# Ten products of a zero tile instead of twenty, and a later, lower-ranked norm chain for half evictions, in a one-layer encoder kernel

## The chip, the core and the metric

One core of a Trainium2 chip runs the whole kernel. The metric is device time in microseconds (us), median of several executions. TensorE (PE) multiplies, VectorE (DVE) and ScalarE (ACT) do the elementwise work, GpSimd (POOL) adds a few tiles and issues accumulating DMAs, SyncE (SP) issues nearly all loads and stores.

## What is computed

One layer with two residual sub-layers, over 512 tokens and 2048 channels. In short:

```python
h = rms_norm(x, norm_gains[0])
parts = split(h @ w_in, 11)             # four head groups: two attentions, a recurrence, a short conv
mixed = concatenate([y_sb, y_df, y_lru, y_sc]) @ w_out
x = x + rms_norm(mixed, norm_gains[1])
h = rms_norm(x, norm_gains[2])
x = x + rms_norm(conv_geglu_ffn(h, w_up, conv_w, w_down), norm_gains[3])
```

`rms_norm` needs, for every token, the sum of squares over all 2048 channels. All data is float32; each product is made of three (or two wider) products of a rounded part `hi` and a rest `lo`.

## The kernel before

Activations lie with channels on the 128 partitions and tokens along the free axis, so a tile holds 128 channels by 512 tokens, or 256 for a half of the tokens. `group` (a helper, lines 133 to 187) multiplies one group of four output blocks by all 2048 input channels, in eight chunks of 256 channels. Each chunk's weights come by one DMA into `w_raw` (three buffers), ACT rounds them into `w_hi` (L106), DVE writes the rest into `w_lo` (L107); `w_hi` and `w_lo` have three buffers each, so the work for chunk c waits for PE to be through with chunk c-3. The PE order is the program order. The order of the other engines is set by a scheduler from the program order and priorities: what stands under `tc.high_priority` (weights, and what `group` calls as `evac`) goes before all else; what an `evac` returns is called by `group` behind it without that priority.

Beside the products, `at(block, fn)` puts small work on a clock that `tick` advances four times in a chunk. PE takes its part of such work exactly at that place.

Places that the change and the prediction speak of:

- **Start.** After twenty products of the zero tile `idle` (L72, two passes each), group 0 of the input projection starts with L128 to L130. Meanwhile ACT and DVE split x (L199, L200) and the first weights. Squares of x (L282) are added up by DVE into `vd` (L284, L286, sixteen tiles); `norm0` (L308) takes the sum through PE at block 28, just ahead of the last chunk of the first group. Tiny instructions on `la_m` and others (L375 to L401) prepare constants on DVE.
- **Output projection.** `out_group` runs groups 0 and 1 over all 512 tokens, then groups 2 and 3 for the first 256 tokens (half 0), then groups 2 and 3 for half 1. PSUM has two pools of four banks, `mm` and `pa`. Its `evac` copies a finished bank out (L968 for full width; L978 and L979 for a half), squares it (L838, POOL adds up) and scales it (L964).
- **The norm chain of a half.** After the last half block, `residual` follows a few blocks later: L852 sums the squares through PE, L207 to L213 make the reciprocal root, L876 multiplies by it, and two accumulating DMAs (L878) and L882 add it to x. Then squares (L894, summed by L896), scalings (L902) and stores of x (L904, on SP), and some blocks later `norm2`: L911 on PE, L207 to L213, L917, and the splits L196/L197 into the input of the up projection of the same half (`up_plain`).

ACT, DVE, POOL and SP each work strictly in their order, so an ACT square (L894) that waits for an accumulating DMA also holds up the weight roundings (L106) behind it.

## Time and profile before

| | us |
|---|---|
| median of 3 executions (1743.55 to 1744.21) | 1743.61 |
| the profiled execution | 1741.86 |
| its span, first to last instruction | 1740.1 |
| PE busy in it | 1730.1 |
| DVE busy | 1253.8 |
| ACT busy | 905.8 |
| POOL busy | 157.8 |

The span is the time between the first and the last instruction on the chip; 1.76 us lie around it. PE is busy in all but 10 us of it. Busy time alone does not say what PE could do in less: a stretch of products is also read by its starts, since ends are modelled.

### The profile page before, as it was taken

The numbers are of one execution on the slowest core, as the hardware profiler recorded it, in microseconds if no ns is written. First come the engines' busy times: TensorE is split into PE (matmuls) and PEld (weight loads), VectorE is DVE, ScalarE is ACT, GpSimd is POOL, SyncE is SP. The second block draws the span as 40 slices with busy tenths as digits, with TensorE's granted clock in tenths as the row PEclk, the third lists the DMA queues.
The fourth block names the chain that finished last, engine by engine and source line by source line (L and its number), as shares of the span: only waits on it lengthen the run. The fifth ranks groups of instructions, "written<-read, shape, count | busy, mean of one in ns | idle before, by whom it ended". The sixth has DMA issues, their size and how long they took to land.

```text
span 1740.1 us, 24385 instructions
## 1 busy us (share of the span) xinstructions
PE 1730.1 (99%) x9168; PEld 1482.5 (85%) x9168; DVE 1253.8 (72%) x1949; ACT 905.8 (52%) x1367; POOL 157.8 (9%) x227
## 2 busy tenths in 40 slices
PE   9999999999999999999999999999999999999998
PEld 8778888888888888899988888888888888888886
DVE  7885587666556425799898988888878887776335
ACT  6443577665334334776655555555555573334342
POOL 0000011100000011100011111111111001110120
PEclk9999999999999999999999999999999999999999
DMA  7224222242223625775789888888888768888322
GB/s 258 84 99 147 92 79 79 79 158 97 85 86 97 230 97 181 233 234 180 208 230 243 236 224 247 225 230 223 228 239 226 210 198 232 217 201 296 102 91 97
DMA packets 96014, 304.43 MB, mean 175 GB/s; under 512 B 10356, under 2 KB 14708, under 8 KB 95896
## 3 DMA queue, kind: packets, MB, share of 16 engines
q1 hardware_dynamic: 79768, 245.19, 42.1%
q0 software_dynamic: 15552, 56.63, 17.4%
q8 instruction: 72, 1.18, 0.3%
q10 hardware_dynamic: 576, 1.05, 0.2%
q14 instruction: 46, 0.38, 0.1%
HBM read 262.45 MB, written 21.24 MB: 163 GB/s over the span
## 4 chain that ended last, share of the span: by engine, by line
PE 92%; DVE 3%; DMA 2%; ACT 2%; issue 1%; SPq 0%; POOL 0%; ACTq 0%; DVEq 0%; POOLq 0%
PE mm L164 32%; PE mm L1113 27%; PE mm L1118 14%; PE pa L164 5%; PE pa L156 2%; PE mm L128 2%; PE mm L130 2%; PE mm L129 2%; PE mm L156 1%; PE pa L611 1%; DMA w_raw<-in_w_out_dram 1%; DVE w_lo L107 1%; DVE vd L286 1%; PE pa L718 1%; ACT w_hi L106 0%
## 5 line engine op out<-in xcount | busy, mean ns | idle before, releaser
L107 DVE TENSOR_TENSOR w_lo<-w_raw,w_hi 128x1024 fp32r<-128x1024 f32 (+1 forms) x195 | 238.5, 1224 | 234.6 <-PE mm L164 117.3
L106 ACT CAST w_hi<-w_raw 128x1024 fp32r<-128x1024 f32 (+1 forms) x195 | 203.5, 1044 | 264.0 <-PE mm L164 174.1
L164 PE MATMUL mm<-a,w_hi 128*128 128x512 f32 (+1 forms) x1504 | 338.2, 375 | 0.0
L164 PEld LDWEIGHTS mm<-a,w_hi 128*128 128x128 f32 x1504 | 266.7, 188 | 50.9 <-issue 1.8
L1113 PE MATMUL mm<-a,w_hi 128*128 128x512 f32 x1088 | 272.6, 392 | 0.0
L1081 ACT CAST w_hi<-w_raw 128x1024 fp32r<-128x1024 f32 x145 | 152.3, 1050 | 196.0 <-PE mm L1113 154.9
L1113 PEld LDWEIGHTS mm<-a,w_hi 128*128 128x128 f32 x1088 | 195.6, 189 | 35.3 <-issue 0.2
L1082 DVE TENSOR_TENSOR w_lo<-w_raw,w_hi 128x1024 fp32r<-128x1024 f32 x145 | 177.0, 1221 | 29.9 <-ACT w_hi L1081 29.3
L164 PE MATMUL mm<-a,w_lo 128*128 128x512 f32 (+1 forms) x752 | 180.4, 377 | 0.0
L1118 PEld LDWEIGHTS mm<-a,w_lo 128*128 128x128 f32 x1088 | 148.4, 190 | 10.6
L1118 PE MATMUL mm<-a,w_lo 128*128 128x256 f32 x1088 | 151.7, 282 | 0.0
L164 PEld LDWEIGHTS mm<-a,w_lo 128*128 128x128 f32 x752 | 131.8, 189 | 22.3
L1113 PE MATMUL mm<-xs,w_hi 128*128 128x512 f32 x576 | 144.3, 392 | 0.2 <-DVE ub L1179 0.2
L1081 ACT CAST w_hi<-mg 128x1024 fp32r<-128x1024 f32 x82 | 85.6, 1044 | 85.0 <-PE mm L1113 82.5
L1113 PEld LDWEIGHTS mm<-xs,w_hi 128*128 128x128 f32 x576 | 103.6, 189 | 19.0 <-DVE ub L1179 0.4
L1082 DVE TENSOR_TENSOR w_lo<-mg,w_hi 128x1024 fp32r<-128x1024 f32 x82 | 100.1, 1220 | 21.4 <-ACT w_hi L1081 21.4
L1113 PE MATMUL mm<-mg,w_hi 128*128 128x512 f32 x352 | 88.1, 392 | 0.0
L1118 PEld LDWEIGHTS mm<-xs,w_lo 128*128 128x128 f32 x576 | 78.6, 190 | 5.6
L1179 DVE TENSOR_TENSOR ub<-ub,mm 128x256 f32<-128x256 f32 x196 | 81.2, 414 | 0.0
L1118 PE MATMUL mm<-xs,w_lo 128*128 128x256 f32 x576 | 80.3, 282 | 0.0
L1281 DVE TENSOR_TENSOR m<-m,mm 128x256 f32<-128x256 f32 x112 | 46.5, 416 | 37.0 <-PE mm L1118 37.0
L1113 PEld LDWEIGHTS mm<-mg,w_hi 128*128 128x128 f32 x352 | 63.3, 189 | 11.3
(332 smaller groups left out, 2709.1 us busy)
## 6 DMA issues: line engine op xcount, KB each, us to landing
w_raw<-in_w_up_dram SPq DMA_DIRECT2D x115, 512.0 KB, 5.3
w_raw<-in_w_in_dram SPq DMA_DIRECT2D x87, 512.0 KB, 3.4
mg<-in_w_up_dram SPq DMA_DIRECT2D x54, 512.0 KB, 4.4
w_raw<-in_w_out_dram SPq DMA_DIRECT2D x48, 512.0 KB, 3.6
w_raw<-in_w_dn_dram SPq DMA_DIRECT2D x32, 512.0 KB, 4.2
mg<-in_w_up_dram POOLq DMA_DIRECT2D x27, 512.0 KB, 7.8
w_raw<-in_w_up_dram POOLq DMA_DIRECT2D x27, 512.0 KB, 8.9
w_raw<-mg POOLq DMA_DIRECT2D x27, 512.0 KB, 6.0
```

Source lines behind the costliest of these rows:

```text
L106: w_split.append(A.copy(out=hi[:, sl], in_=raw[:, sl]))
L107: V.tensor_tensor(out=lo[:, sl], in0=raw[:, sl], in1=hi[:, sl].bitcast(F32), op=ALU.subtract)
L128: T.matmul(ps, lhsT=sh, rhs=mh, start=first, stop=False)
L129: T.matmul(ps, lhsT=sh, rhs=ml, start=False, stop=False)
L156: T.matmul(pss[u][:, 0:256] if low else pss[u].rearrange("p (a t) -> p a t", a=2), lhsT=(wh, wl)[low][:, kk, us], rhs=both[k][:, 0, ts] if ...
L164: T.matmul(pss[u], lhsT=a, rhs=b, start=c == 0 and kk == 0 and not low and i == 0, stop=False)
L1081: w_split.append(A.copy(out=by4(hi), in_=v))
L1082: V.tensor_tensor(out=by4(lo), in0=v, in1=by4(hi).bitcast(F32), op=ALU.subtract)
L1113: T.matmul(ps.rearrange("p (a t) -> p a t", a=2), lhsT=hi[:, k * P:(k + 1) * P], rhs=tops[name][k], start=first and k == 0, stop=False, **kw)
L1118: T.matmul(ps[:, 0:256], lhsT=lo[:, k * P:(k + 1) * P], rhs=tops[name][k][:, 0], start=False, stop=k == 7, **kw)
L1179: taken.append(V.tensor_tensor(out=t, in0=t, in1=ps[:, 256:512], op=ALU.add))
L1281: V.tensor_tensor(out=t, in0=t, in1=part, op=ALU.subtract if i else ALU.add)
```

## The change

The program multiplies the zero tile ten times, not twenty. Group 1 of the output projection puts its sums into the four `pa` banks, not into the `mm` banks that group 0 has just used. For half blocks only the copy and the addition (L978, L979) stay in the high-priority part; squaring and scaling move into a function that `evac` returns and that is ranked in program order. `residual` comes 8 blocks after the last block, not 6, and `norm2` 44 blocks after `residual`, not 43, with the squares and scalings between them at the same distance from `residual` as before.

```diff
-    for _ in range(20):
+    for _ in range(10):
         T.matmul(ps, lhsT=idle, rhs=idle, start=True, stop=True)
...
-            at(clock[0] + 43, lambda: norm2(hf, acc))
+            at(clock[0] + 44, lambda: norm2(hf, acc))
...
                     sum_of(m, ps)
-                    last = ss1[hfs[0]].add(m)
-                    A.activation(out=m, in_=m, func=AF.Copy, scale=gain(1, k))
-                    if last:
-                        at(clock[0] + 6, lambda: residual(hfs[0]))
+
+                    def more():
+                        last = ss1[hfs[0]].add(m)
+                        A.activation(out=m, in_=m, func=AF.Copy, scale=gain(1, k))
+                        if last:
+                            at(clock[0] + 8, lambda: residual(hfs[0]))
+                    return more
...
         for g in range(2):
-            out_group(g, (0, 1), ALL, mm_tile)
+            out_group(g, (0, 1), ALL, pa_tile if g else mm_tile)
```

The scheduler answers with another order in three places. (Lines after L963 carry numbers that are two or three higher in the changed kernel.)

DVE, ahead of `norm0`, the last additions of squares into `vd`; L107 is the rest of the tenth chunk's weights (the second chunk of group 1). Before:

```order
L286 TENSOR_TENSOR vd<-vd,t_446 128x512
L386 TENSOR_TENSOR la_m<-la_m,la_q 128x4
L286 TENSOR_TENSOR vd<-vd,t_485 128x512
L387 TENSOR_SCALAR la_m<-la_m 128x4
L286 TENSOR_TENSOR vd<-vd,t_488 128x512
L386 TENSOR_TENSOR la_m<-la_m,la_q 128x4
L107 TENSOR_TENSOR w_lo<-w_raw,w_hi 128x1024
```

Now:

```order
L286 TENSOR_TENSOR vd<-vd,t_436 128x512
L386 TENSOR_TENSOR la_m<-la_m,la_q 128x4
L107 TENSOR_TENSOR w_lo<-w_raw,w_hi 128x1024
L286 TENSOR_TENSOR vd<-vd,t_475 128x512
L387 TENSOR_SCALAR la_m<-la_m 128x4
L286 TENSOR_TENSOR vd<-vd,t_478 128x512
L386 TENSOR_TENSOR la_m<-la_m,la_q 128x4
```

The tenth chunk's rest stood behind the last addition and now stands ahead of the last two; the rests of the two chunks before it have moved forward among the additions in the same way.

ACT, evicting group 2 of half 1 while PE works on group 3 of that half; L106 rounds that group's weights, the last one shown being its third chunk's. Before:

```order
L894 ACTIVATE f_5953<-xs 128x512
L978 COPY mg<-mm 128x256
L902 ACTIVATE mg<-xs,par 128x256
L978 COPY mg<-mm 128x256
L838 ACTIVATE q_5968<-mg 128x256
L838 ACTIVATE q_5978<-mg 128x256
L964 ACTIVATE mg<-mg,par 128x256 x2
L838 ACTIVATE q_5993<-mg 128x256
L978 COPY mg<-mm 128x256
L964 ACTIVATE mg<-mg,par 128x256
L106 CAST w_hi<-w_raw 128x1024
```

Now:

```order
L981 COPY mg<-mm 128x256
L894 ACTIVATE f_5934<-xs 128x512
L981 COPY mg<-mm 128x256
L894 ACTIVATE f_5937<-xs 128x512
L981 COPY mg<-mm 128x256
L106 CAST w_hi<-w_raw 128x1024
L981 COPY mg<-mm 128x256
L838 ACTIVATE q_5952<-mg 128x256
L838 ACTIVATE q_5962<-mg 128x256
L966 ACTIVATE mg<-mg,par 128x256
L106 CAST w_hi<-w_raw 128x1024
```

The second L106 of the new rows rounds that third chunk; four squares, two scalings and a copy have moved behind it or between it and the rounding of the chunk before.

ACT, evicting the last half blocks (group 3 of half 1) while PE runs the first chunks of the up projection; the four L838 are squares that the second half's `residual` (L852) waits for. Before:

```order
L838 ACTIVATE q_6227<-mg 128x256
L838 ACTIVATE q_6236<-mg 128x256
L964 ACTIVATE mg<-mg,par 128x256 x2
L838 ACTIVATE q_6245<-mg 128x256
L978 COPY mg<-pa 128x256
L964 ACTIVATE mg<-mg,par 128x256
L106 CAST w_hi<-w_raw 128x1024
L838 ACTIVATE q_6254<-mg 128x256
```

Now:

```order
L838 ACTIVATE q_6217<-mg 128x256
L981 COPY mg<-pa 128x256
L966 ACTIVATE mg<-mg,par 128x256
L981 COPY mg<-pa 128x256
L106 CAST w_hi<-w_raw 128x1024
L196 CAST a_94<-mg 128x2x256
L838 ACTIVATE q_6226<-mg 128x256
L106 CAST w_hi<-w_raw 128x1024
L196 CAST a_94<-mg 128x2x256
L966 ACTIVATE mg<-mg,par 128x256
L838 ACTIVATE q_6235<-mg 128x256
L838 ACTIVATE q_6244<-mg 128x256
```

Three of the four squares now stand behind one or two weight roundings and the splits L196 of the next products' input.

## Rows read from the trace of the kernel before

**Rows 1.** The page, part 1: busy us, share of the span, instructions.

```profile
PE 1730.1 (99%) x9168; PEld 1482.5 (85%) x9168; DVE 1253.8 (72%) x1949; ACT 905.8 (52%) x1367; POOL 157.8 (9%) x227
```

**Rows 2.** Waits of PE: waiting line, releaser, us in total, times, longest.

```profile
PE pa L156 <- ACT w_hi L106: 1.4, 1, 1.4
...
PE mm L156 <- ACT q L838: 0.7, 1, 0.7
PE pa L852 <- ACT q L838: 0.4, 1, 0.4
PE pa L156 <- DVE w_lo L107: 0.4, 1, 0.4
PE pa L308 <- DVE vd L286: 0.3, 1, 0.3
```

**Rows 3.** Groups by line, zero-tile passes in 1.6:4.6, then in 5.1:7.3: busy, mean ns.

```profile
L72 PE MATMUL pa<-idle 128*128 128x128 f32 x16 | 3.8, 431 | 1.2 <-DVE la_m L384 1.2
...
L72 PE MATMUL pa<-idle 128*128 128x128 f32 x22 | 2.6, 275 | 0.0
```

**Rows 4.** Timeline of the start: start us, us, engine, line, operation, count, idle before.

```profile
7.42 0.48 PE L128 MATMUL mm<-a,w_hi 128*128 128x512 f32 x1
...
12.96 0.39 PE L164 MATMUL mm<-a,w_hi 128*128 128x512 f32 x1
...
4.96 0.62 ACT L106 CAST w_hi<-w_raw 128x512 fp32r<-128x512 f32 x1 [0.22 <-DMA w_raw<-in_w_in_dram]
...
11.26 1.41 DVE L200 SCALAR_TENSOR_TENSOR a<-t,par,a 128x512 fp32r<-128x512 f32 x2
```

**Rows 5.** Timeline around `norm0` (L308), PE and DVE.

```profile
43.79 1.98 PE L164 MATMUL mm<-a,w_lo 128*128 128x512 f32 x8
46.08 1.12 PE L308 MATMUL pa<-vd,con 128*128 128x512 f32 x2 [0.31 <-DVE vd L286]
...
45.33 0.69 DVE L286 TENSOR_TENSOR vd<-vd,t 128x512 f32<-128x512 f32 x1
...
46.01 1.22 DVE L107 TENSOR_TENSOR w_lo<-w_raw,w_hi 128x1024 fp32r<-128x1024 f32 x1
```

**Rows 6.** Timeline of PE, first three chunks of group 2, half 0.

```profile
651.16 1.52 PE L156 MATMUL mm<-a,w_hi 128*128 128x512 f32 x6
...
654.88 2.00 PE L156 MATMUL mm<-a,w_hi 128*128 128x512 f32 x8
...
657.67 2.00 PE L156 MATMUL mm<-a,w_hi 128*128 128x512 f32 x8
```

**Rows 7.** Timeline of groups 2 and 3 of half 1: PE chunks, ACT, POOL's accumulating DMA.

```profile
722.85 2.00 PE L156 MATMUL pa<-a,w_hi 128*128 128x512 f32 x8
...
727.19 2.10 PE L156 MATMUL pa<-a,w_hi 128*128 128x512 f32 x8 [1.38 <-ACT w_hi L106]
...
730.73 2.00 PE L156 MATMUL pa<-a,w_hi 128*128 128x512 f32 x8
...
713.84 0.63 ACT L894 ACTIVATE s<-xs 128x512 f32<-128x512 f32 x1 [4.67 <-DMA xs<-mg]
...
726.11 1.03 ACT L106 CAST w_hi<-w_raw 128x1024 fp32r<-128x1024 f32 x1
...
706.99 1.02 POOL L878 DMA_DIRECT2D xs<-mg  x1 [7.88 <-DMA w_raw<-in_w_out_dram]
```

**Rows 8.** Timeline of the second chunk of the up projection, with the second `residual`.

```profile
748.48 1.12 PE L164 MATMUL mm<-a,w_hi 128*128 128x256 f32 x8
...
754.19 2.08 PE L164 MATMUL mm<-a,w_hi 128*128 128x256 f32 x16
...
751.29 0.41 ACT L838 ACTIVATE q<-mg 128x256 f32<-128x256 f32 x1
```

**Rows 9.** Stretches at the end: us, PE and other busy (x), PEclk, DMA.

```profile
1736.00:1738.00 2.00, 0.00 (x0) 0.00 (x0) 0.00 (x0) 0.00 (x0) 0.00 (x0) 1.00 1.05 405
1739.00:1740.00 1.00, 0.00 (x0) 0.00 (x0) 0.00 (x0) 0.00 (x0) 0.00 (x0) 0.50 0.03 8
```

## Prediction

> **What bounds the kernel now.** I read the page first: PE is busy 1730.1 of 1740.1 us [rows 1], so what the change can win lies almost wholly in the 10 us in which PE does nothing. Then the waits of PE, which say where those are [rows 2]: five waits inside the program, 1.4, 0.7, 0.4, 0.4 and 0.3 us. The rest is the 1.2 us before the first product and the 5 us of output behind the last one, which the change does not touch. Last the timelines around each wait, by starts of chunks and not by busy time, because a stalled stretch is longer than its idle row says. A chunk of a half takes 657.67 - 654.88 = 2.79 us when nothing stalls it [rows 6]. Against that: the first chunk of group 2, half 0, takes 654.88 - 651.16 = 3.72, so 0.93 is lost there [rows 6]; in group 3 of half 1 two chunks take 727.19 - 722.85 = 4.34 and 730.73 - 727.19 = 3.54, so 1.55 + 0.75 = 2.30 are lost [rows 7]. The whole prize beyond the start is thus about 3.2 us at these two places, 0.2% of the time, plus what the start gives.
>
> **The ten products.** Zero-tile passes come some 0.21 us apart at first (16 in a stretch of 3.0 us, 431 ns each) and some 0.11 us apart later (22 in 2.2 us, 275 ns each) [rows 3]: half clock, then full clock. Twenty products are forty passes; of the twenty that stay, about 17 run at the slow pace, so PE is through at about 5.3, not 7.4. The first rounded weights are there at 4.96 + 0.62 = 5.58 [rows 4], so the first real product can start at about 5.7 instead of 7.42. This is not kept in full: the second chunk needs the rest of the fourth x tile, which DVE finishes at 11.26 + 1.41 = 12.67 [rows 4]. Its fourth product started before at 12.96 + 3 x 0.23 = 13.65 (0.23 is (12.96 - 7.42) / 24) and can start now at 12.7. PE is 0.9 us earlier from there on.
>
> **But `norm0` comes later.** L308 needs the last addition into `vd`. It waited only 0.31 for it [rows 2, 5]; now the tenth chunk's rest (L107) stands ahead of the last two additions, and that L107 waits for PE itself: its buffer comes free when PE has finished the low products of the seventh chunk (43.79 + 1.98 = 45.77, and L107 started at 46.01) [rows 5]. With PE 0.9 earlier it starts at 45.1, takes 1.22, then one addition with a tiny instruction (46.01 - 45.33 = 0.68) and the last addition (0.69): 47.7, and L308 right behind, where it was 46.08 [rows 5]. **So PE leaves this point 1.6 us later than before, not 0.9 earlier.** Does DVE reach that L107 in time? The two rests before it also moved forward and wait for PE's fifth and sixth chunk; adding up additions at 0.6, tiny instructions at 0.1 and rests at 1.14 from there, DVE arrives at 45.0, just in time. If the start gave nothing, the price would be 2.5; if DVE did not have to wait for PE, about 1.2.
>
> **Group 1 on the other banks.** The 0.69 idle before the fourth bank of group 2 ended with ACT's squares of group 1's last bank, and those now sit in `pa`. `pa` is next wanted by group 3, 23 us later, so nothing takes the wait's place there. The next rounding also follows in time behind the same squares. Worth -0.93, with -0.69 (the idle row alone) as the lower bound of the gain.
>
> **Squares and norms of the halves.** What ends the 1.4 us wait is the rounding at 726.11, ready at 727.14 for a PE that is due at 722.85 + 2.79 = 725.64 [rows 7]. It is late because ACT stood still for 4.67 us until the accumulating DMA landed at 713.8 [rows 7] and then had squares, scalings and copies in front. I followed the new orders of ACT and DVE with the durations of these rows. `residual` moves two blocks, 2 x 2.79 / 4 = 1.4 us, and one more weight rest (1.14) stands ahead of the second L876, so the DMA starts at about 709.2, not 706.99, and lands after its old 6.85 at 716.1. The last chunk of group 2 is now rounded ahead of ACT's wait (at 710.9), so the later landing does not reach PE there. Behind it come two squares (1.1), a scaling (0.4), the first chunk's rounding (ready 718.6, due 720.1), and so on: the third chunk's rounding starts at 724.15 and is ready at 725.2, 0.4 before PE needs it, its rest 0.5 before. Both waits go: -2.30. SP's queue is passed too: the stores of x (L904) wait for that DMA, but one more weight load now stands ahead of the first of them, and the loads behind land 4 us or more before their roundings.
>
> How much is given back? PE now comes 2.3 us earlier to work of ACT and DVE that did not get shorter. At the second `residual`, L852 waits for four squares, the last of which was at 751.29 [rows 8]; before, the chunk took 754.19 - 748.48 = 5.71 [rows 8], of which I put 0.7 down to the wait, and now three of the squares stand behind roundings and splits: I get 751.1 for the last, and a wait of 1.1. Two chunks of the next group later, the third chunk's rounding stands behind four evictions, three scalings and squares: about 0.8 late. `norm2`, three blocks later against the products, has its sums a microsecond early and its first split tile about when PE wants it. I take half: -1.15, with 0 and -2.3 as the ends.
>
> **The sum.** +1.6 - 0.93 - 1.15 = -0.5 us. Against the profiled execution that is 1741.86 - 0.5 = 1741.4; this execution lies 1.75 below the median, so **1743.2** against 1743.61. What a measurement can tell from no change is about 0.2%, 3.5 us; this is far inside it. The own range of this case is 1742.2 to 1744.2.
>
> **Rivals.** *The start is kept.* If the last additions reach PE no later than PE reaches them (DVE idle where I have it busy), PE stays 0.9 earlier and even loses the old wait of 0.3 to 0.5: -1.3 - 0.93 - 1.15 = -3.4, 1740.2. For it speaks that DVE is one of four engines with slack on the page; against it that the L107 in question has a named buffer that PE holds until 45 us.
>
> *The cover in the second half holds to the end* (no new waits behind it): +1.6 - 0.93 - 2.3 = -1.6, 1742.0. *It does not form at all* (DMA later than its old 6.85, the third rounding late again): +1.6 - 0.93 = +0.7, 1744.3. The margin of 0.4 us decides between them, and it is the thinnest one in my sum.
>
> *The clock falls while PE waits for `norm0`: slower.* PE would stand idle there from about 44.9 to 47.7, 2.8 us, where it stood 0.31. In the trace the granted clock is 1.00 in 1736 to 1738 and 0.50 in 1739 to 1740, after the products have ended [rows 9], so standing still does bring it down; the trace shows no pause near 2.8 us, so whether this is enough is open. [...] Price from rows: at the start the slow pace held for about 3.7 us (16 or so passes of 0.21) [rows 3], in which a product takes twice its time, so about 1.8 us are lost, and the sum becomes +1.3: 1744.9. It decides if the pause reaches what the clock bears; with a start that gives nothing and no cover in the second half on top, it ends at +4, 1747.5. The same at the start (real products at half clock from 5.7 on) costs at most the 0.9 that the start gives, since DVE's tile at 12.67 holds PE anyway.
>
> **How the numbers follow.** Forecast 0.44; start kept 0.12; cover to the end 0.12; no cover 0.18; clock falls 0.14. The likeliest gives 1743.2. The range leaves out the outer parts of the start kept and of the clock: 1740.5 to 1746.0. Faster than 1740.1 takes the start kept with a good second half: 0.08. Slower than 1747.1 takes the fall of the clock with a bad one, or a stall that I did not find: 0.06. The rest, 0.86, is within 0.2%.
>
> **What would show it.** Right: in the changed kernel L308 starts at about 47.7 with a wait of 2 to 3 us on DVE's `vd`; no wait of L156 on L838 near 652; no wait of L156 on L106 in the third chunk of group 3, half 1; L852 of the second half waits about 1 us on L838; PE's granted clock stays at 1.00. Wrong: a wait at L308 under 1 us (then the start is kept), a rounding of that third chunk behind PE, a stretch with granted clock 0.50 near 48 us, or new waits in the seven-product units of the up projection, whose order on SP and POOL also moved by a place or two and which I cost at nothing, because PE waits there hardly at all before.

## The result, and the profile after

The changed kernel takes 1750.37 us (median of 5, 1748.12 to 1752.44) against 1743.97 (5 runs, 1743.55 to 1744.98): ratio 1.0033, 95% interval 1.0021 to 1.0046, so 3.7 to 8.0 us more. Run once more beside three other kernels it took 1750.19, ratio 1.0043 (1.0029 to 1.0056). The prediction said 1743.2, with 1746.0 as its upper end: wrong, and on the wrong side of "no change".

The profiled execution took 1748.12, its span is 1746.4. Its page, part 1, and the waits of PE (columns as in [rows 2]):

```profile
PE 1731.5 (99%) x9148; PEld 1481.4 (85%) x9148; DVE 1255.8 (72%) x1949; ACT 904.8 (52%) x1367; POOL 160.8 (9%) x227
```

```profile
PE pa L308 <- DVE vd L286: 2.8, 1, 2.8
PE mm L1116 <- DVE ub L1182: 1.7, 2, 1.5
PE mm L164 <- DVE a L197: 1.4, 2, 0.7
PE pa L72 <- DVE la_m L384: 1.2, 1, 1.2
PE pa L852 <- ACT q L838: 0.8, 1, 0.8
PE mm L911 <- DVE s L896: 0.7, 1, 0.7
```

The two waits of [rows 2] that were to go are gone (L156 on L838, L156 on L106). In their place stand two that the prediction named, the 2.8 us at L308 and 0.8 at L852 (1.1 forecast), and three that it put at nothing: L1116 on L1182, L164 on L197, and L911.

The most useful reading is none of these lines but a subtraction: the start of a product in one trace less the start of the same product (the n-th of its line) in the trace of before. That is how late PE is there, and the stretches between two places show where it was lost. In us, at times of the kernel before; "end" is the difference of the spans, and the last column is the median against before's in the same set, with the runs' interval. The names are those of the runs under Experiments.

| kernel | 13.5 | 52 | 660 | 732 | 748 | 800 | 852 | end | median, us (95%) |
|---|---|---|---|---|---|---|---|---|---|
| changed | -1.3 | +2.7 | +1.7 | -0.6 | +1.4 | +4.4 | +6.0 | +6.3 | +6.4 (3.7 to 8.0) |
| changed, again | -1.1 | +1.5 | +0.6 | -1.7 | +1.1 | +3.9 | +5.6 | +6.7 | +6.1 (5.1 to 9.8) |
| p_ten | -0.6 | +3.6 | +3.6 | +2.6 | +2.6 | +3.9 | +4.0 | +4.7 | +4.5 (3.0 to 7.0) |
| a_twenty | +0.4 | +0.4 | -0.6 | -2.9 | -1.1 | -0.1 | +1.5 | +2.9 | +1.2 (0.2 to 3.3) |
| a_fill | -0.9 | +1.7 | +0.7 | -1.6 | -0.6 | +0.1 | +1.7 | +2.7 | +1.7 (0 to 3.0) |
| a_wide | -0.5 | +2.1 | +1.2 | -1.2 | -0.3 | +1.7 | +3.3 | +5.1 | +4.3 (2.8 to 6.3) |
| a_s8 | -0.1 | -0.5 | -1.5 | -3.8 | -3.0 | -0.9 | +0.7 | +1.9 | +1.0 (-0.3 to 2.8) |
| v_s8 | -0.7 | -1.2 | -2.1 | -2.0 | -1.9 | -0.4 | -0.5 | +2.4 | 0.0 (-1.4 to 1.6) |
| p_pa | +0.8 | +0.8 | -0.2 | -0.2 | -0.2 | -0.1 | -0.2 | +0.7 | +0.6 (-0.9 to 2.1) |
| p_more | +1.0 | +1.0 | +0.9 | 0.0 | 0.0 | +3.7 | +3.5 | +5.7 | +1.4 (-0.5 to 2.6) |
| p_late | +0.7 | +0.7 | +0.7 | +0.6 | +0.6 | +1.7 | +3.1 | +7.4 | +2.1 (0.9 to 4.0) |
| a_early | -0.5 | +3.7 | +2.7 | +1.8 | +1.8 | +5.5 | +5.3 | +6.1 | +4.5 (2.8 to 5.9) |
| a_z2 | +0.8 | +3.2 | +2.2 | -0.1 | +0.7 | +2.9 | +4.6 | +7.7 | +6.4 (3.7 to 8.5) |
| a_z7 | -0.7 | +1.9 | +0.9 | -1.4 | -0.6 | +1.8 | +3.4 | +5.8 | +6.0 (3.3 to 7.5) |
| a_z13 | -0.9 | +3.2 | +2.2 | -0.1 | +1.1 | +2.5 | +4.1 | +5.6 | +5.6 (3.7 to 6.6) |
| a_store0 | -0.8 | +1.8 | +0.8 | -1.5 | +0.7 | +3.0 | +4.7 | +5.6 | +6.6 (4.7 to 8.9) |

The lateness is of one execution, the median of 5 to 11. The execution of before that all are compared with took 1741.86, 1.3 to 2.2 us less than the medians of before in the sets; so an "end" of about +2 stands for no difference. Where the two columns differ by more or less than that, the execution is a quick or a slow one of its kernel (p_late's and p_more's are the slowest of 11; in them 4 and 2 us are lost behind 852). Before itself scatters from 1740.9 to 1747.3 over 28 runs on one chip.

**The pause.** DVE and PE in the changed kernel around `norm0`; to be laid beside [rows 5] (columns: start us, us, engine, line, operation, tiles, shapes, count, and in brackets PE's idle time before it and what ended it):

```profile
44.78 1.22 DVE L107 TENSOR_TENSOR w_lo<-w_raw,w_hi 128x1024 fp32r<-128x1024 f32 x1
45.91 0.68 DVE L286 TENSOR_TENSOR vd<-vd,t 128x512 f32<-128x512 f32 x1
46.52 0.16 DVE L387 TENSOR_SCALAR la_m<-la_m 128x4 f32<-128x4 f32 x1
46.63 0.69 DVE L286 TENSOR_TENSOR vd<-vd,t 128x512 f32<-128x512 f32 x1
...
47.38 2.08 PE L308 MATMUL pa<-vd,con 128*128 128x512 f32 x2 [2.78 <-DVE vd L286]
48.47 1.42 PE L128 MATMUL mm<-a,w_hi 128*128 128x512 f32 x1
```

The rest stands ahead of the last two additions, and L308 starts at 47.38, where 47.7 was forecast. The pause is 2.77 or 2.78 us long in all eight traces that have it, whether PE arrives 1.2 us early, as here, or 0.8 late, as in a_z2: it moves along with PE. DVE does not idle ahead of the rest at 44.78. It waits for PE two rests earlier, at the eighth chunk's (1.7 us in p_ten, 1.2 in a_z2), and is busy without a break from there. So PE leaves the pause 2.5 us later than before, less what it was early. And the granted clock (PEclk, third column from the right in stretches of 1 us) falls in this execution, with the first product behind the pause taking 1.42 us:

```profile
46.00:47.00 1.00, 0.00 (x0) 0.00 (x0) 1.00 (x3) 0.00 (x0) 0.00 (x0) 0.96 0.02 4
47.00:48.00 1.00, 0.62 (x1) 0.50 (x2) 0.90 (x5) 0.00 (x0) 0.00 (x0) 0.50 0.83 254
48.00:49.00 1.00, 1.00 (x3) 0.34 (x1) 0.83 (x6) 0.00 (x0) 0.00 (x0) 0.50 0.66 262
49.00:50.00 1.00, 1.00 (x3) 0.66 (x2) 0.34 (x3) 0.45 (x1) 0.00 (x0) 0.50 0.01 4
```

In the second execution of the same program it does not, and PE is 1.2 us earlier behind the pause (+1.5, not +2.7, at 52):

```profile
47.00:48.00 1.00, 0.38 (x1) 0.30 (x2) 0.93 (x4) 0.00 (x0) 0.00 (x0) 1.00 0.67 180
48.00:49.00 1.00, 1.00 (x4) 0.57 (x3) 0.83 (x6) 0.16 (x1) 0.00 (x0) 1.00 0.84 340
```

**The second half.** PE's rows with an idle time before them, from 742 us on:

```profile
747.01 2.04 PE L164 MATMUL mm<-a,w_hi 128*128 128x256 f32 x15 [0.68 <-DVE a L197]
754.47 1.13 PE L852 MATMUL pa<-q,con 128*128 128x256 f32 x4 [0.76 <-ACT q L838]
779.28 2.18 PE L164 MATMUL pa<-a,w_hi 128*128 128x256 f32 x16 [0.17 <-ACT w_hi L106]
789.34 2.17 PE L164 MATMUL pa<-a,w_hi 128*128 128x256 f32 x16 [0.30 <-ACT w_hi L106]
795.99 0.39 PE L130 MATMUL pa<-a,w_lo 128*128 128x256 f32 x1 [0.33 <-DVE w_lo L107]
799.72 2.06 PE L164 MATMUL mm<-a,w_hi 128*128 128x256 f32 x15 [0.70 <-DVE a L197]
853.11 2.11 PE L1116 MATMUL mm<-a,w_hi 128*128 128x512 f32 x8 [1.53 <-DVE ub L1182]
```

In the kernel before the same stretch has one such wait, 0.4 us at L852 [rows 2]. From 732 (-0.6) to 852 (+6.0) PE loses 6.6 us: the 2.3 that it won in group 3, and 4.3 more.

### The profile page after: what moved, and what is told of

Its sections match the earlier page's. It is cut to its first block, busy times and chain, and to the rows that moved or that the text cites. A ratio compares the mean times of both kernels' runs of the same rounds, so it can differ in the third digit from the quotient of the medians.

```text
span 1746.4 us, 24342 instructions
## 1 busy us (share of the span) xinstructions
PE 1731.5 (99%) x9148; PEld 1481.4 (85%) x9148; DVE 1255.8 (72%) x1949; ACT 904.8 (52%) x1367; POOL 160.8 (9%) x227
## 3 DMA queue, kind: packets, MB, share of 16 engines
q8 instruction: 72, 1.18, 0.3%
## 4 chain that ended last, share of the span: by engine, by line
PE 90%; DVE 5%; issue 3%; DMA 1%; ACT 1%; POOL 0%; ACTq 0%; DVEq 0%; POOLq 0%; SPq 0%
PE mm L164 29%; PE mm L1116 26%; PE mm L1121 13%; PE pa L164 4%; PE pa L156 2%; PE mm L156 2%; PE mm L128 2%; PE mm L130 2%; PE mm L129 2%; DVE w_lo L107 1%; PE pa L611 1%; PE pa L718 1%; DMA w_raw<-in_w_up_dram 0%; DVE a L197 0%; PE pa L128 0%
## 5 line engine op out<-in xcount | busy, mean ns | idle before, releaser
L107 DVE TENSOR_TENSOR w_lo<-w_raw,w_hi 128x1024 fp32r<-128x1024 f32 (+1 forms) x195 | 239.4, 1228 | 234.5 <-PE mm L164 88.8
L106 ACT CAST w_hi<-w_raw 128x1024 fp32r<-128x1024 f32 (+1 forms) x195 | 203.4, 1045 | 269.4 <-PE mm L164 148.0
L164 PE MATMUL mm<-a,w_hi 128*128 128x512 f32 (+1 forms) x1392 | 312.4, 375 | 1.6 <-DVE a L197 1.4
L164 PEld LDWEIGHTS mm<-a,w_hi 128*128 128x128 f32 x1392 | 245.5, 188 | 49.1 <-issue 1.8
L1116 PE MATMUL mm<-a,w_hi 128*128 128x512 f32 x1088 | 272.6, 392 | 1.5 <-DVE ub L1182 1.5
L1116 PEld LDWEIGHTS mm<-a,w_hi 128*128 128x128 f32 x1088 | 195.6, 189 | 36.7 <-DVE ub L1182 1.7
L164 PE MATMUL mm<-a,w_lo 128*128 128x512 f32 (+1 forms) x696 | 166.9, 376 | 0.0
L1121 PEld LDWEIGHTS mm<-a,w_lo 128*128 128x128 f32 x1088 | 148.4, 190 | 10.6
L1116 PE MATMUL mm<-xs,w_hi 128*128 128x512 f32 x576 | 144.3, 392 | 0.2 <-DVE ub L1182 0.2
L164 PEld LDWEIGHTS mm<-a,w_lo 128*128 128x128 f32 x696 | 121.4, 189 | 20.2
L1116 PEld LDWEIGHTS mm<-xs,w_hi 128*128 128x128 f32 x576 | 103.6, 189 | 19.0 <-DVE ub L1182 0.4
L1116 PE MATMUL mm<-mg,w_hi 128*128 128x512 f32 x352 | 88.1, 392 | 0.0
L1182 DVE TENSOR_TENSOR ub<-ub,mm 128x256 f32<-128x256 f32 x196 | 81.4, 416 | 0.0
L1116 PEld LDWEIGHTS mm<-mg,w_hi 128*128 128x128 f32 x352 | 63.3, 189 | 11.3
```

The lines of the kernel that those rows point to most:

```text
L106: w_split.append(A.copy(out=hi[:, sl], in_=raw[:, sl]))
L107: V.tensor_tensor(out=lo[:, sl], in0=raw[:, sl], in1=hi[:, sl].bitcast(F32), op=ALU.subtract)
L164: T.matmul(pss[u], lhsT=a, rhs=b, start=c == 0 and kk == 0 and not low and i == 0, stop=False)
L1116: T.matmul(ps.rearrange("p (a t) -> p a t", a=2), lhsT=hi[:, k * P:(k + 1) * P], rhs=tops[name][k], start=first and k == 0, stop=False, **kw)
L1121: T.matmul(ps[:, 0:256], lhsT=lo[:, k * P:(k + 1) * P], rhs=tops[name][k][:, 0], start=False, stop=k == 7, **kw)
L1182: taken.append(V.tensor_tensor(out=t, in0=t, in1=ps[:, 256:512], op=ALU.add))
```

## Experiments

Fifteen runs, one of them the changed kernel again; medians and lateness are in the table above.

**One part alone.** p_ten: the kernel before with the one line of the start.

```diff
-    for _ in range(20):
+    for _ in range(10):
```

> The kernel before with ten zero products instead of twenty and nothing else. Theory (pause and clock): the rest of the tenth chunk stands ahead of the last two additions again, L308 starts at about 47.4 instead of 46.08 behind a wait of about 2.8 us, the granted clock falls to 0.50 there for about 3.4 us, and PE is about 2.6 us late from 51 us on; the three stalls near 653 and 727 stay as before. Ends at +2.6: 1746.6 us against 1743.97 of before, between 1745.5 and 1747.5. Rival (the start is worth its 0.9 us and the pause is harmless): 1743.1. Rival (the pause costs its wait but the clock belongs to something else in the changed kernel): +1.3, 1745.3, and granted clock 1.00 throughout.

Measured 1748.27, above the range given. The pause is there, 2.78 us, the clock falls, this time while PE is already at work (49 to 52 us), and PE is 3.6 us late at 52. So this line alone carries most of the loss, 4.5 of 6.4 us. PE's row at L308, then a stretch of 1 us:

```profile
48.11 1.38 PE L308 MATMUL pa<-vd,con 128*128 128x512 f32 x2 [2.78 <-DVE vd L286]
```

```profile
49.00:50.00 1.00, 1.00 (x3) 0.62 (x2) 0.83 (x6) 0.41 (x1) 0.00 (x0) 0.50 0.36 139
```

a_twenty is the counterpart, the changed kernel with twenty again.

```diff
-    for _ in range(10):
+    for _ in range(20):
```

> The changed kernel with twenty zero products again; everything else as changed. Theory (the ten products make two thirds of the loss, the later halves the rest): the additions into vd come ahead of the tenth chunk's rest as before, L308 waits 0.3 us, the clock stays at 1.00, and PE is within 1 us of its old times until 650; then 0.9 won at 653, up to 2.3 won at 727, and 3 to 5 lost between 735 and 850: 1745 us, between 1744 and 1746.5. Rival (all of the loss is the pause): 1743 or below. Rival (the halves make most of it, the pause little): 1748 to 1749.

Measured 1745.26: the theory's number. L308 waits 0.3, the clock stays up, +0.4 at 52. The ten products cost about 5 us in the one direction (1750.2 to 1745.3, in one set) and 4.5 in the other.

p_pa: group 1 on the `pa` banks, nothing else.

```diff
-            out_group(g, (0, 1), ALL, mm_tile)
+            out_group(g, (0, 1), ALL, pa_tile if g else mm_tile)
```

> The kernel before with group 1 on the other banks and nothing else. Theory: the wait of 0.69 us (0.93 by the chunk) near 653 goes, nothing takes its place before 700; behind 700 PE is 0.9 us earlier to work that did not get shorter, and keeps half of it or all: 1743 to 1743.8 against 1744 of before, within what can be measured. Rival (the later banks are busy in turn and a new wait comes up before 700): 1744 to 1744.5.

Measured 1744.39, ratio 1.0003 (0.9995 to 1.0012): no difference. Yet in the trace the 1.0 us is won at 653 (+0.8 to -0.2) and kept to 860 us: the theory's trace, without the rival's new wait, and too small to be seen in the time.

p_more: the squares and scalings in ordinary rank, with 6 and 43 blocks as before.

```diff
-                    last = ss1[hfs[0]].add(m)
...
+                    def more():
+                        last = ss1[hfs[0]].add(m)
+                        A.activation(out=m, in_=m, func=AF.Copy, scale=gain(1, k))
+                        if last:
+                            at(clock[0] + 6, lambda: residual(hfs[0]))
+                    return more
```

p_late: 8 and 44 blocks with the high rank of before.

```diff
-            at(clock[0] + 43, lambda: norm2(hf, acc))
+            at(clock[0] + 44, lambda: norm2(hf, acc))
...
-                        at(clock[0] + 6, lambda: residual(hfs[0]))
+                        at(clock[0] + 8, lambda: residual(hfs[0]))
```

> The kernel before with the squares and scalings of half blocks in ordinary rank and nothing else (residual after 6 blocks, norm2 after 43, as before). Theory (what costs is the later norms, not the rank): the roundings of group 3 pass the squares, the stall of 2.3 us near 727 shrinks by 1 to 2 us, L911 of the second half starts no later than its old 782.99, and the unbroken DVE work behind it ends no later than before: 1742 to 1744 us, -0 to -2 against 1743.97. Rival (the rank costs: squares behind roundings make residual and all behind it late): L852 of the second half waits 2 us or more, and the time is 1746 to 1750.

> The kernel before with residual after 8 blocks and norm2 after 44, and nothing else (squares and scalings keep their high rank). Theory (the later norms cost): norm2 of the second half comes three blocks of 0.7 us later, 2.1 us, and DVE works without a break from its first instruction behind L911 until some 57 us later, so that delay reaches the first product that waits for L1182/L1179 near 850; weight loads behind the later stores of x add up to 2 us: 1746 to 1748.5 us, +2 to +4.5. Rival (the rank costs, not the later norms): 1743.5 to 1744.5.

Measured 1745.22 (1.0006, not clear of 1) and 1745.89 (1.0014, 1.0005 to 1.0023). The first lies between the ranges of its theory and its rival, the second just under its theory's. Each trace shows a price of its own. With the rank alone, the squares come behind the roundings, and `residual` after 6 blocks is too early for them. PE stands 2.1 us and 0.3 us in the middle of L852, and the clock falls there (PE's rows, then stretches of 1 us):

```profile
749.85 0.59 PE L852 MATMUL pa<-q,con 128*128 128x256 f32 x2
752.57 1.13 PE L852 MATMUL pa<-q,con 128*128 128x256 f32 x4 [2.13 <-ACT q L838]
753.99 0.73 PE L852 MATMUL pa<-q,con 128*128 128x256 f32 x2 [0.28 <-ACT q L838]
```

```profile
755.00:756.00 1.00, 1.00 (x6) 1.00 (x6) 1.00 (x2) 1.00 (x3) 0.00 (x0) 0.50 0.92 303
756.00:757.00 1.00, 1.00 (x6) 1.00 (x6) 1.00 (x4) 1.00 (x3) 0.00 (x0) 0.50 0.48 184
```

That is 3.7 us between 748 and 760, and a_early repeats it. With the later norms alone, the wait for L1179 near 850 appears (+1.5 between 846 and 852). So the two belong together: the 8 blocks give the squares the time that the lower rank takes, and the late start of the second half's norms is what they cost.

a_early: the changed kernel with 6 and 43 blocks.

```diff
-            at(clock[0] + 44, lambda: norm2(hf, acc))
+            at(clock[0] + 43, lambda: norm2(hf, acc))
...
-                            at(clock[0] + 8, lambda: residual(hfs[0]))
+                            at(clock[0] + 6, lambda: residual(hfs[0]))
```

> The changed kernel with residual after 6 blocks and norm2 after 43, as before: ten products, other banks and the ordinary rank of squares and scalings remain. Theory (the later norms cost 2 to 3 us, through norm2 of the second half, behind which DVE works without a break for 57 us): the wait of 1.5 us for L1182 near 852 goes, 1747 to 1748.5. Rival (the rank makes them late): 1749.5 to 1751, as in the changed kernel.

Measured 1748.28, the theory's number, but not for its reason alone: the wait at 852 is gone (5.5 to 5.3), and L852 with the clock has taken its place (+3.7 between 748 and 760).

**The pause covered or taken away.** a_fill puts eleven products of the zero tile into it:

```diff
         def norm0():
             ps = pa_tile()
+            for _ in range(11):
+                T.matmul(ps[:, 0:P], lhsT=idle, rhs=idle, start=True, stop=True)
             T.matmul(ps, lhsT=ones, rhs=ssum, start=True, stop=True)
```

> The changed kernel with eleven more zero products put into the pause, just ahead of L308 (2.4 us of work for PE while it would stand idle; what PE waits for is the same). Theory (the pause brings the clock down): L308 still starts at about 47.4, the granted clock stays at 1.00, the first products behind it run at their usual pace, and PE is 1.3 us earlier than in the changed kernel from 51 us on: 1749.1 us against 1750.4. Since the clock is then never low, its runs should also lie closer together than the 4.3 us over which those of the changed kernel are spread, within about 1 us. Rival (the shorter warm-up at the start, not the pause, brings the clock down): clock falls all the same, 1750.4. Rival (the spread has another source, DMA for one): gain of 1.3 us but the spread of 4 us stays.

PE's rows in the pause, then stretches of 1 us:

```profile
44.87 2.62 PE L309 MATMUL pa<-idle 128*128 128x128 f32 x22
47.80 1.12 PE L310 MATMUL pa<-vd,con 128*128 128x512 f32 x2 [0.31 <-DVE vd L286]
48.36 0.80 PE L128 MATMUL mm<-a,w_hi 128*128 128x512 f32 x1
```

```profile
47.00:48.00 1.00, 0.69 (x6) 0.50 (x5) 0.96 (x5) 0.00 (x0) 0.00 (x0) 1.00 0.55 111
48.00:49.00 1.00, 1.00 (x4) 0.48 (x3) 0.83 (x6) 0.00 (x0) 0.00 (x0) 1.00 1.01 389
```

Measured 1745.52, and the clock is never down. The expected gain was 1.3; it is 4.8, though PE gets to L128 no earlier than in the changed kernel. Its 11 runs lie within 2.0 us, not 1, and all below all ten of the changed kernel. The clock explains a part of this surplus at most: each run's mean granted clock is on record to three places, and it is 0.9987 over the ten runs of the changed kernel, 0.9997 in a_fill, 0.9993 in a_s8 below. One fall takes 0.001 off (0.999 in the first profile of the changed kernel, 1.000 in the second), so this is 0.6 to 1 fall for each run, an estimate of 1 to 1.5 us. And the second execution of the changed kernel has no fall, is within 0.1 us of a_fill up to 731, and still ends 3.9 us behind it. That is followed up below.

a_s8 takes the pause away at its root. The squares of x are issued one block earlier, which puts all additions into `vd` ahead of the two rests:

```diff
-            at(max(9 + k // 2, clock[0] + 1), squares)
+            at(max(8 + k // 2, clock[0] + 1), squares)
```

> The changed kernel with the squares of x issued one block earlier (from block 8, not 9), which puts all sixteen additions into vd ahead of the ninth and tenth chunks' rests on DVE. Theory (the order on DVE makes the pause, the pause brings down the clock): L308 no longer waits, the clock stays at 1.00, and the 0.5 to 1.3 us won at the start are kept to 640 us; the losses of the second half stay: 1743 to 1744.5 us, 6 less than the changed kernel. Rival (the rests, now behind the additions, are late for group 1, and PE waits there instead): a wait of 1 us or more on w_lo between 48 and 56, 1745 to 1747.

PE's rows at the same place:

```profile
43.88 1.98 PE L164 MATMUL mm<-a,w_lo 128*128 128x512 f32 x8
45.70 1.02 PE L308 MATMUL pa<-vd,con 128*128 128x512 f32 x2
46.15 0.79 PE L128 MATMUL mm<-a,w_hi 128*128 128x512 f32 x1
```

L308 no longer waits, PE waits nowhere between 10 and 660 us, and the time is 1745.03: 5.2 us back, with ten products and the same number of PE instructions. So the loss of the ten products comes with the order on DVE, not with the shorter warm-up. It ends 0.5 above the range given; from 732 to 852 it loses 4.5 us, a_fill 3.3.

v_s8: the kernel before with ten products, `pa` for group 1 and the earlier squares; its half blocks are untouched.

```diff
-    for _ in range(20):
+    for _ in range(10):
...
-            at(max(9 + k // 2, clock[0] + 1), squares)
+            at(max(8 + k // 2, clock[0] + 1), squares)
...
-            out_group(g, (0, 1), ALL, mm_tile)
+            out_group(g, (0, 1), ALL, pa_tile if g else mm_tile)
```

> Ten zero products, the squares of x one block earlier, group 1 on the other banks, and the half blocks as in the kernel before (high rank, residual after 6 blocks, norm2 after 43). Theory: no wait at L308, no wait near 653, the stall of 2.3 us in group 3 of the second half is back, and no losses between 735 and 850: PE 1 us early at 640, 2 early at 660, and so to the end, but for what the weights' DMAs cost by chance: 1742 us, 1 to 2 below before and 1.5 below the run with the later halves. Rival (being early only moves into later waits, since DVE and ACT set the times from 700 on): 1743.5 to 1744.5, as before.

Measured 1744.01, ratio 1.0000 (0.9992 to 1.0009): the rival. PE is 2.1 us early at 660 and 0.4 at 800; at the end of this execution nothing is left of it (+2.4, which is about the median of before). No kernel here beats the one before.

**Where the other 2 us come from.** after_again ("changed, again" in the tables): the changed kernel, unaltered.

> The changed kernel once more, unaltered, on the chip of the next three, to be compared with them and to have a second profile of it. Theory (pause and clock are the same every time, part of the late loss is chance): L308 starts at about 47.4 or 48 behind a wait of 2.8 us, granted clock 0.50 for about 3.4 us near 47 to 52, PE 2.5 to 3.7 us late at 52 us; between 735 and 800 us it loses again, by waits for weights behind the accumulating DMAs and stores, but not in the same places: 1749 to 1751 us. Rival (the profile read so far was an exception): no fall of the clock, 1746 us.

Measured 1750.19; the clock did not fall, against the theory, and the time was the same. From 732 to 748 us a_fill loses 1.0 us and this one 2.8. ACT's rows show what differs, the rounding of the same weights, and behind each the issue of these weights (us from issue to landing at the end of the line). In a_fill:

```profile
732.08 1.04 ACT L106 CAST w_hi<-w_raw 128x1024 fp32r<-128x1024 f32 x1
```

```profile
w_raw<-in_w_out_dram SPq DMA_DIRECT2D x1, 512.0 KB, 4.3
```

In after_again:

```profile
734.05 1.05 ACT L106 CAST w_hi<-w_raw 128x1024 fp32r<-128x1024 f32 x1 [2.01 <-DMA w_raw<-in_w_out_dram]
```

```profile
w_raw<-in_w_out_dram SPq DMA_DIRECT2D x1, 512.0 KB, 6.4
```

Both were issued at 727.4 to 727.5. It is the sixth of the eight chunks of group 3, and everything ACT has behind it (scalings, L207, the splits of `norm2`) is 2.0 us later. A packet of PE's program, 16384 bytes, is on its way at 729.86 in after_again and takes 1.99 us; in a_fill it passes at 725.14. There are 72 such packets in a run (the page: "q8 instruction: 72, 1.18, 0.3%"). The Trainium skill, "Runtime: NRT & Kernel Launch", section "Instruction fetch mechanics", says that an engine fetches its program by its own DMA queue in blocks of 16 KiB, 256 instructions, at a cost that is mostly hidden; that fits the packets (an estimate by its 256: PE's 18,296 products and weight loads make 71.5 blocks), and the question was whether it is hidden here. Five kernels were made for it, all from the changed one. a_wide covers the pause with 16 PE instructions instead of 44:

```diff
             ps = pa_tile()
+            for _ in range(4):
+                T.matmul(ps[:, 0:CH], lhsT=idle, rhs=con, start=True, stop=True)
             T.matmul(ps, lhsT=ones, rhs=ssum, start=True, stop=True)
```

a_z2, a_z7 and a_z13 have two, seven and thirteen zero products, with the order on ACT, DVE, POOL and SP unchanged:

```diff
-    for _ in range(10):
+    for _ in range(2):
```

a_store0 issues the stores of x of the first half later, which changes SP's order alone:

```diff
-            with tc.issue_after(w_load[-1].ins):
-                nc.sync.dma_start(out=x1_d[q][:, hf], in_=xs[q][hf])
+            def store():
+                with tc.issue_after(w_load[-1].ins):
+                    nc.sync.dma_start(out=x1_d[q][:, hf], in_=xs[q][hf])
+            if hf == 0:
+                at(clock[0] + 20, store)
+            else:
+                store()
```

> The changed kernel with the pause ahead of L308 covered by four products of the zero tile with 384 constant columns (about 0.65 us each, 2.6 us together), where the run with eleven narrow products had 44 instructions more and this one has 16. The order of all other engines is the same in the three. What is tested is why eleven narrow products gained 4.7 us, when a second profile of the changed kernel shows no fall of the clock and is equal to 0.1 us with theirs until 731 us. Theory (program blocks): PE's program comes by DMA in blocks of 16384 bytes, 72 of them, one every 16 to 30 us; the number of PE instructions sets at which point of the computation a block is fetched; in the changed kernel one comes at 730 to 731 us, in the flight of the weights issued at 727.5, which then take 5.8 and 6.4 us, not 4.3 as with the eleven products (block at 725.1). With 16 instructions the block comes about 1.5 us earlier than in the changed kernel, at 728 to 729.5, still in that flight: the load takes 5.5 us or more, and the run is 1747.5 to 1749.5, that is, it gains the clock alone. Rival (the clock, which the cover holds up in every execution): 1745 to 1746, like the eleven products.

> The changed kernel with two zero products at the start, not ten; same order on every other engine, and 32 PE instructions fewer. The pause ahead of L308 stays. Theory (program blocks): the blocks are fetched some 3 us later against the computation, near 733 and 789, behind the flights of the weights issued at 727.5 (4.3 to 5 us then) and 780.6 (6.2 to 6.6, not 7.5): 1746 to 1748 although the pause and its clock are as before. Rival (clock): no gain, 1750 or more, since the shorter warm-up can only make PE slower at the start. Either way the start itself should cost nothing at the end, as L308 waits for DVE.

> The changed kernel with seven zero products, not ten: 12 PE instructions fewer, same order on every other engine. Theory (blocks): the block comes about 1.1 us later than in the changed kernel, near 731 to 732.5, in the last 3 us of the flight of the same load, which takes 5 us or more. Rival (chance): no relation. By both the pause ahead of L308 stays and the time is 1749.5 to 1751; with PE late at the start, as with two products, up to 1 us more.

> The changed kernel with thirteen zero products, not ten: 12 PE instructions more, same order on every other engine, pause and clock as they are. Theory (which block of PE's program falls into which load): the block near 730 to 731 comes about 1.1 us earlier, 729 to 730; the load issued near 727.5 to 728.5 takes 5 us or more if the block comes in the last 4 us of its flight, as in both executions of the changed kernel. Rival (chance from one execution to the next, whatever the block): 4.1 to 6.4 us without relation to it. Time 1749.5 to 1751 by both: the pause is the same.

> The changed kernel with the four stores of x of the first half (L904) twenty blocks, 14 us, later; only SP's order changes, every other engine's is the same, and the pause ahead of L308 stays. Theory (the weights issued near 727 are late because they share the DMA engines with these stores): the load issued near 727 to 728 lands after 3.5 to 4.3 us instead of 5.8 and 6.4, PE loses 0.8 us or less between 732 and 748 instead of 2.0 and 2.8, and the time is 1 to 2 us below the changed kernel: 1748.5 to 1749.5. Rival (the store is not what makes them late): same load 5.5 us or more, 1750 to 1751.

That load in all ten traces with 8 and 44 blocks and the lower rank, so with the same order here, with the packet of PE's program in its flight (time behind the issue, duration) and what PE lost from 732 to 748:

| kernel | flight, us | packet: at, took | lost, us |
|---|---|---|---|
| a_wide | 4.11 | +0.7, 0.88 | 0.9 |
| a_fill | 4.32 | none | 1.0 |
| a_z2 | 4.44 | none | 0.8 |
| a_s8 | 4.58 | +1.0, 1.36 | 0.8 |
| a_z13 | 4.63 | +1.5, 0.88 | 1.1 |
| a_z7 | 4.70 | +2.8, 0.99 | 0.9 |
| a_twenty | 5.08 | 2.1 us ahead, 2.85 | 1.7 |
| changed | 5.80 | +2.7, 0.98 | 2.0 |
| a_store0 | 5.90 | +1.0, 2.83 | 2.2 |
| changed, again | 6.43 | +2.3, 1.99 | 2.8 |

What this shows: PE's loss follows the flight (up to 4.7 us: 0.8 to 1.1; above 5: 1.7 to 2.8), and in each of the three executions with a packet of about 2 us or more the flight was over 5. What it doesn't show is the theory as it was put, that the place of the packet decides: a_wide and a_z7 have one in flight and are quick, with "5.5 or more" and "5 or more" forecast; a_wide's 1748.07 lies in the theory's range by luck, by losses elsewhere. The number of zero products does not steer it either (1750.17, 1749.17, 1748.69 with two, seven and thirteen, against 1750.3): the first is the rival's number, the others lie a little under the range of both. And a_store0 (1749.70) was a poor test: SP reached the later stores at 724 and 728, still beside the load. How long a packet takes looks like chance of the execution, and whether a long packet makes the load late or both have another cause isn't shown.

**Why the covered or removed pause gives back 5 us, where 52 us shows 1.5 to 2.7, stays open**. In the two traces of the changed kernel most of the rest is lost between 732 and 800 us (5.0 and 5.6 us, for 1.7 to 2.9 in a_fill, a_twenty and a_s8), where weights land late; but a_z2, a_z7 and a_z13, which have the pause too, lose only 2.6 to 3.2 there, so no run ties it to the pause. a_wide, with cover and 2.2 us of gain rather than 4.8, says that cover alone doesn't do it.

## Why the prediction was wrong, step by step

Two of its three terms failed. The ten products, +1.6, measured +4.5 (p_ten) and 4.9 (changed again less a_twenty). The halves, -1.15, measured about +1.0 (a_s8 less v_s8, their intervals overlapping). Group 1, -0.93, was right by the trace; the time doesn't show it.

**The ten products: the time at L308 right, the price too small; the first step that failed.** 47.38 for 47.7, a wait of 2.78 for "2 to 3", and PE late by 1.5 us without the clock, for 1.6. The start gained as said (-1.3 at 13.5 for -0.9; -0.5 to -1.1 in the six other traces with ten products and the squares in their old place), and "if the start gave nothing, the price would be 2.5" holds in all eight traces with the pause; only the rest that waits for PE is the eighth chunk's, not the tenth's. The rival of the clock, at 0.14, was the term that failed here: a pause of 2.78 us at L308 stands in eight of the traces, and the clock fell in four (changed, p_ten, a_early, a_z13), which made PE 1.4 to 1.6 us later for the forecast 1.8. It should have had half the chance. The worst case of that rival, "+4", adds up to +3.4 from its own terms (2.5 - 0.93 + 1.8). The Trainium skill, "TensorE: Matmul & The Clock Gate", section "Why this matters for your kernels", warns of long idle gaps between bursts of products; here the clock fell at one and the same gap in four traces of eight. With both, the ten products are worth 1.5 to 3.6 us at 52, and 4.5 to 5 in the time; the rest is the open point above.

**Group 1 on the other banks: right**, 1.0 us for 0.93.

**The stall in group 3 of half 1: right.** Both waits go, and PE wins 2.3 us between 720 and 732 in the changed kernel, a_fill, a_twenty and a_s8 alike, with the margin that the prediction called thin.

**What is given back: wrong, and the second step that failed.** "I take half: -1.15, with 0 and -2.3 as the ends" bounds the loss by the gain. It is not bounded: from 732 to 852 PE lost 6.6 and 7.2 us in the changed kernel, 4.4, 3.3 and 4.5 in a_twenty, a_fill and a_s8, where the pause is absent or covered, and 4.2 to 4.8 in a_z2, a_z7 and a_z13, where it stands. The single steps under it:

- L852 of the second half: 0.76 for a forecast of 1.1, of which 0.42 were there before. Right.
- "`norm2` has its sums a microsecond early": wrong. L911 waits 0.7 for DVE's last sum (L896) of the first half, because the DMA landed at 717.6 and ACT's squares (L894) were spread between roundings.
- "The loads behind land 4 us or more before their roundings": wrong. ACT waited for weights 1.15 us at 734 and 1.99 at 788, loads that shared the time with stores of x (landing at 731.6 and 786.4). (Such waits were there before, 0.79 at 733 and 1.94 at 762, but none cost PE a wait.)
- "New waits in the seven-product units, which I cost at nothing": the largest single wait, 1.5 us at L1116. The three blocks (8 for 6, 44 for 43) were priced for the first half alone. In the second half, ACT's L207 of `norm2`, first in before and then in the changed kernel, is 7.0 us later. L911 ahead of it is 4.5 us later on PE, of which the three blocks are 2.1 and the rest is PE's own lateness; ACT's wait for weights comes on top:

```profile
785.92 1.03 ACT L106 CAST w_hi<-w_raw 128x1024 fp32r<-128x1024 f32 x1
786.85 0.47 ACT L207 ACTIVATE f<-mm,eps 128x256 f32<-128x256 f32 x1
```

```profile
788.24 1.05 ACT L106 CAST w_hi<-w_raw 128x1024 fp32r<-128x1024 f32 x1 [1.99 <-DMA w_raw<-in_w_up_dram]
789.19 2.10 ACT L902 ACTIVATE mg<-xs,par 128x256 f32<-128x256 f32 x5
...
793.88 0.47 ACT L207 ACTIVATE f<-mm,eps 128x256 f32<-128x256 f32 x1
```

Behind it DVE has norms, splits and sums without a break to 853 us (third pair of columns, busy us of 10 with its count; then DVE's row at the end):

```profile
800.00:810.00 10.00, 10.00 (x85) 9.99 (x85) 10.00 (x14) 7.87 (x14) 0.00 (x0) 1.00 0.58 191
...
840.00:850.00 10.00, 10.00 (x72) 9.43 (x72) 9.97 (x13) 4.42 (x7) 1.75 (x2) 1.00 0.83 269
```

```profile
852.64 0.41 DVE L1182 TENSOR_TENSOR ub<-ub,mm 128x256 f32<-128x256 f32 x1
```

and PE waits for its end, 1.53 at L1116. Before, DVE was as busy and just in time there; the same sum ended at 847.06 and PE, not waiting, started at 847.12:

```profile
846.64 0.42 DVE L1179 TENSOR_TENSOR ub<-ub,mm 128x256 f32<-128x256 f32 x1
847.12 2.11 PE L1113 MATMUL mm<-a,w_hi 128*128 128x512 f32 x8
```

The delay is passed on almost whole: the first instruction of this chain (L209) starts at 794.38 for 788.12, 6.3 us later, the last at 852.64 for 846.64, 6.0 later. "PE waits there hardly at all" was read as slack; it was a chain without slack. This wait, 1.4 to 1.5 us near 850, stands in each trace with 8 and 44 blocks, p_late's included, and in none with 6 and 43.

By medians the halves cost little in sum, 1.0 us with the pause gone (a_s8 against v_s8); the larger part of what the prediction missed in time is the pause and what follows it.

**The median.** The prediction added the 1.75 us by which the profiled execution lay under the median. The traces tell where part of that came from: with twenty products the first real one starts at 7.42 in before [rows 4], and 0.4 to 1.0 later in the four other traces with the start unchanged, because the zero passes keep their slow pace longer. Passes in one microsecond (x behind PE's busy time) in before, then in p_more; PEclk reads 1.00 in both rows, so here the pace alone shows it:

```profile
5.00:6.00 1.00, 1.00 (x11) 1.00 (x11) 0.92 (x2) 1.00 (x2) 0.00 (x0) 1.00 0.73 184
```

```profile
5.00:6.00 1.00, 1.00 (x6) 1.00 (x6) 0.87 (x2) 0.96 (x2) 0.00 (x0) 1.00 0.86 281
```

## To carry to other kernels

When a change moves a chain later, follow the engine behind it to the first place where it is idle, and not to the first wait: 59 us of unbroken DVE work pass a delay on almost whole, and "hardly any wait" may mean just in time. What a change can lose is not bounded by what it wins; and an early start is worth nothing ahead of a wait for another engine, while the pause that it opens there can cost TensorE's clock besides. Where two edits are each other's cover, as the rank and the 8 blocks here, judge them as one.

## What was not expected of the hardware

- A pause of 2.78 us brought the granted clock to 0.50 in four of eight executions, and one of 2.1 us, with 0.3 more behind a few products, in the middle of L852 in two of two (p_more, a_early); two waits of 2.0 us behind 880 us (p_more, v_s8) and those of 1.5 us did not. The same program does it in one execution and not in the next.
- The pace of the first products doubles at different times from one execution to the next, which alone moves the start by 1.0 us.
- Weight loads of the same size, issued at the same point of the same program order, landed after 4.1 to 6.4 us.
- Being early is not kept: v_s8 is 2.1 us ahead at 660, 0.5 at 852, and measures as before.
